# A hybrid attention layer on one core: PSUM banks of the level products given back 1.2 planned microseconds later, and the order of small products that follows

## The chip, the cores and the metric

The kernel runs on one core of one Trainium2 chip. The time is device microseconds for one execution. Three runs of the kernel before gave 207.26, 206.81 and 206.92 us, median 206.92. One more execution was profiled: it took 207.39 us, and its span (first to last instruction of the trace) is 205.6 us, so 1.8 us lie around the span.

## The reference

One decoder layer on 256 tokens of width 1024. The input is normalised (RMS) and multiplied by a wide matrix `w_in` whose columns are split into parts; two branches follow and are merged by gates:

```
h = rms_norm(x, norm_in_g[layer])
proj = jnp.einsum('bsd,de->bse', h, w_in[layer])
(mq, mk, mv, mgate, gq, gk, gv, ggate, gfg, ga, gb) = jnp.split(proj, split_pts, axis=-1)
...
oa = moba_attention(qa, ka, va)          # 8 heads of 64, causal softmax over 256 keys
oa = oa * silu(mgate);  ya = oa @ w_proj_a
...
ob = gla_chunked(qb, kb, vb, gdec)       # 4 heads, decay per channel, chunks of 64
ob = rms_norm(ob) * silu(ggate);  yb = ob @ w_proj_b
merged = sigmoid(ga + b0) * ya + sigmoid(gb + b1) * yb
out = rms_norm(x + merged @ w_out)
```

With 256 tokens there is one block of keys, so the first branch is plain causal attention. In the second branch the weight between two positions of a chunk is a sum over channels of q, k and a decay, which the kernel builds from six levels of block products (block sizes 32 down to 1) and the diagonal.

## The kernel before, in words

Large products. All weights come as 512 KB chunks. `load_to` (L170) issues a chunk's DMA into one of 5 raw buffers, `split_to` (L183) splits it on ScalarE into a high part (`hi`, L193) and on VectorE into the rest (`lo`, L194), each in one of 5 buffers, and `three` (L724) multiplies high by high, high by low and low by high. Splits run 4 chunks ahead of TensorE, loads up to 8. The groups are computed in a fixed order: mg, gg, gqk, mq, mk, mv, gv, ga, gb, then pa and pb (the two projections), then po (the output). Products of gv are 512 columns wide, those of ga and gb 256.

Small products. Two Python generators run beside the large groups. `gla()` (L368) makes the second branch: the level products `a` (L459, in two passes over the levels, the loop of L439), then `b` (L477), `c` (L492), `o` (L506) and the transposes `tr` (L528). `scores()` (L539) is started four times, once for each pair of heads: products `sc` (L548), mask and maximum on VectorE (L556), exponentials on ScalarE (L563), division on VectorE (L569), transposes `pt` (L577), a copy back on ScalarE (L581), and the products `pv` (L594).

The order. The program that is built is one fixed list of instructions for each engine; no scheduler changes it. A planned clock (L139) is advanced by each large product, and a generator that yields a number is resumed when that many planned microseconds, times 0.9, have passed. Two rules decide when a small product may be written into the list. First, `together()` (L331) holds small products back until several ask or one has waited long enough (L662), so that they stand in blocks between large products. Second, the small products share four PSUM banks, counted in `room` (L318): `take("small", 2)` (L320) holds a generator until two are free, `give` (L325) frees them. This count exists at planning time alone. On the chip a bank is handed on by semaphores: the first product in a bank waits until the engine that read its last contents is done.

What reads a bank: `a` is copied out on VectorE by predicated copies (L468), `sc` by VectorE (L556), `b` by ScalarE (L482), `c` by ScalarE (L495), `pt` by ScalarE (L581), `o` by ScalarE and VectorE (L512, L520).

Of the kernel before, what the change touches and what calls it, by code (L numbers as in the profile page):

```python
# [130 lines left out]
def layer(ctx, tc, x, xT, columns, weights, w_fg2, b_fg, gla_g, norm_f_g, rope, causal, sums, masks, out):  # L131
# [9 lines left out]
    def mm(out, lhsT, rhs, start, stop):  # L141
        nc.tensor.matmul(out, lhsT, rhs, start=start, stop=stop)  # L142
        n = out.free_size() / 2400
        clock[0] += n if rhs.dtype == F32R else 4 * n
# [14 lines left out]
    def small(name):  # L159
        return bank(name, "small", 4)  # L160
# [159 lines left out]
    def take(tag, n=1):  # L320
        while room[tag] < n:
            yield 0.3
        room[tag] -= n

    def give(tag, n=1):  # L325
        room[tag] += n
# [4 lines left out]
    def together(weight=1):  # L331
        me = [weight, clock[0]]
        company["ask"].append(me)
        while not company["open"]:
            yield 0
        company["ask"].remove(me)
# [31 lines left out]
    def gla():  # L368
# [44 lines left out]
        def halves(ap, n, which):  # L413
            return ap.rearrange("p g (b h j) -> p g b h j", h=2, j=n)[:, :, :, which, :]

        def upper(ap, l):
            return ap.rearrange("p (b h j) -> p b h j", h=2, j=LEVELS[l])[:, :, 1, :]
# [21 lines left out]
        for levels in ((0, 1, 2, 3), (4, 5, NL)):  # L439
            yield from take("small", 2)  # L440
            yield from together(2)
            banks = [small(f"a{r}") for r in range(2)]
            at, cuts = 0, []
            for l in levels:
                width = CH // 2 if l < NL else CH
                cuts.append([bk[:, at:at + 4 * width].rearrange("p (g t) -> p g t", t=width) for bk in banks])
                at += 4 * width
            for l, a in zip(levels, cuts):
                for g, (t, ct) in enumerate(order):
                    for par in range(2):  # L450
                        c = 2 * t + par
                        for r in range(2):
                            rows = halves64[r]
                            if l < NL:
                                lhs = EX[rows, ct, l, c * CH:(c + 1) * CH]
                                rhs = upper(lhs, l)
                            else:
                                lhs, rhs = gkT[rows, ct, c * CH:(c + 1) * CH], gqT[rows, ct, c * CH:(c + 1) * CH]
                            mm(a[r][halves64[par], g, :], lhs, rhs, start=True, stop=True)  # L459
            yield 0.6  # L460
            for l, a in zip(levels, cuts):
                for r in range(2):
                    to, mask, new = ATr[:, r], masksb[:, l:l + 1, :].to_broadcast([P, 4, CH]), a[r]
                    if l < NL:
                        j = LEVELS[l]
                        to, mask = halves(to, j, 1), halves(mask, j, 1)
                        new = new.rearrange("p g (b j) -> p g b j", j=j)
                    nc.vector.copy_predicated(to, mask, new)  # L468
            give("small", 2)
            yield 1  # L470
        ready.add("levels")
        yield from take("small", 2)
        yield from together()
# [197 lines left out]
    def wait_for(*names):  # L671
        while not all(n in ready for n in names):
            wait(0.3)

    start_side(gla())
    start_side(attention())

# [225 lines left out]
```

## Time and profile before

| | |
|---|---|
| median of three runs | 206.92 us (206.81 to 207.26) |
| profiled execution | 207.39 us, span 205.6 us |
| TensorE (PE) busy | 195.0 us, 95% of the span |
| VectorE (DVE) busy | 141.2 us, 69% |
| ScalarE (ACT) busy | 123.4 us, 60% |
| GpSimd (POOL) busy | 38.1 us, 19% |
| mean DMA rate | 177 GB/s |
| chain that ended last: PE | 58% of the span |

A matmul row lasts from its start to the modelled end of a pipelined operation, so rows of PE overlap, and a busy share of 95% doesn't say how fast one follows the other. The distance from one start to the next does. A wait is shown in brackets behind a row, with the engine and line that ended it. A matmul of plain fp32 shows as two rows, so four products `sc` are eight rows.

### The profile page before, as it was taken

What the parts mean: (1) busy time and instruction counts of PE and PEld (TensorE: products, weight loads), DVE (VectorE), ACT (ScalarE), POOL (GpSimd) and SP (SyncE); (2) the same over time, 40 slices, a digit from 0 to 9 for tenths busy, and PEclk for the clock granted to TensorE, in tenths of its full rate; (3) what the DMA queues carried; (4) which work ended last, traced back from release to release, by engine and by line L of the source; (5) the groups of instructions that cost most, each with busy time, mean ns of one, the idle gap of its engine ahead of it and who ended that gap; (6) DMA issues with size and microseconds to landing.
All of it is one profiled execution on the core that took longest, in us unless ns stands there. A gap on an engine that the chain in (4) does not pass through costs nothing.

```text
span 205.6 us, 4197 instructions
## 1 busy us (share of the span) xinstructions
PE 195.0 (95%) x1666; PEld 179.0 (87%) x1666; DVE 141.2 (69%) x259; ACT 123.4 (60%) x205; POOL 38.1 (19%) x31
## 2 busy tenths in 40 slices
PE   7999978999999999989999999999999999999970
PEld 3899968899999887867789999999999999989870
DVE  3776278969655999989567448945284959755471
ACT  6685657865999956058774729756436553552251
POOL 2000034800412579002000001100010060420011
PEclk9999999999999999999999999999999999999997
DMA  6999986484546446542333372756363683500022
GB/s 175 332 407 398 346 319 205 141 296 148 168 138 205 125 183 204 175 139 100 108 102 100 119 256 69 287 198 207 102 202 108 207 298 110 204 0 5 0 102 102
DMA packets 12245, 36.44 MB, mean 177 GB/s; under 512 B 1457, under 2 KB 2882, under 8 KB 12226
## 3 DMA queue, kind: packets, MB, share of 16 engines
q1 hardware_dynamic: 11794, 35.64, 51.2%
q10 hardware_dynamic: 432, 0.54, 0.7%
q8 instruction: 13, 0.21, 0.4%
q14 instruction: 6, 0.05, 0.1%
HBM read 35.12 MB, written 1.05 MB: 176 GB/s over the span
## 4 chain that ended last, share of the span: by engine, by line
PE 58%; DVE 12%; ACT 11%; DMA 8%; issue 6%; SPq 2%; POOL 1%; POOLq 0%; DVEq 0%; ACTq 0%
PE ga L142 11%; PE gb L142 11%; PE po L142 8%; PE gqk L142 6%; PE pa L142 5%; PE pb L142 5%; DVE lo L194 5%; DMA xt<-in_x_dram 5%; ACT hi L193 4%; ACT z L705 3%; DMA first<-in_weights_dram 3%; PE mq L142 3%; PE gv L142 2%; DVE EX L422 2%; ACT EX L405 2%
## 5 line engine op out<-in xcount | busy, mean ns | idle before, releaser
L194 DVE TENSOR_TENSOR lo<-raw,hi 128x1024 fp32r<-128x1024 f32 (+1 forms) x56 | 70.7, 1270 | 30.2 <-ACT hi L193 30.1
L193 ACT CAST hi<-raw 128x1024 fp32r<-128x1024 f32 (+1 forms) x56 | 57.9, 1048 | 21.6 <-PE po L142 6.0
L142 PE MATMUL ga<-xh,hi 128*128 128x256 f32 x64 | 18.1, 283 | 0.0
L142 PE MATMUL gb<-xh,hi 128*128 128x256 f32 x64 | 18.1, 282 | 0.0
L142 PE MATMUL gb<-xl,hi 128*128 128x256 f32 x64 | 17.9, 279 | 0.0
L142 PE MATMUL gb<-xh,lo 128*128 128x256 f32 x64 | 17.9, 279 | 0.0
L142 PE MATMUL ga<-xh,lo 128*128 128x256 f32 x64 | 17.8, 278 | 0.0
L142 PE MATMUL ga<-xl,hi 128*128 128x256 f32 x64 | 17.8, 278 | 0.0
L142 PE MATMUL po<-hi,ml 128*128 128x512 f32 (+1 forms) x40 | 13.9, 347 | 0.0
L142 PE MATMUL po<-lo,mh 128*128 128x512 f32 (+1 forms) x40 | 13.8, 346 | 0.0
L142 PE MATMUL po<-hi,mh 128*128 128x512 f32 (+1 forms) x40 | 13.7, 343 | 0.0
L142 PEld LDWEIGHTS ga<-xh,hi 128*128 128x128 f32 x64 | 12.1, 189 | 0.5 <-issue 0.5
L516 POOL TENSOR_TENSOR s<-s,mhalf 128x4 f32<-128x4 f32 x2 | 2.3, 1170 | 54.6 <-DVE s L515 54.6
L563 ACT ACTIVATE sm<-sm,mx 128x128 f32<-128x128 f32 (+1 forms) x16 | 7.1, 443 | 8.7 <-DVE mx L558 8.6
L142 PEld LDWEIGHTS gb<-xh,lo 128*128 128x128 f32 x64 | 12.1, 189 | 0.0
L142 PEld LDWEIGHTS gb<-xh,hi 128*128 128x128 f32 x64 | 12.1, 189 | 0.0
L142 PEld LDWEIGHTS ga<-xl,hi 128*128 128x128 f32 x64 | 12.0, 188 | 0.0
L142 PEld LDWEIGHTS gb<-xl,hi 128*128 128x128 f32 x64 | 12.0, 188 | 0.0
L142 PEld LDWEIGHTS ga<-xh,lo 128*128 128x128 f32 x64 | 12.0, 188 | 0.0
L709 POOL TENSOR_TENSOR kT<-kT,z 128x512 f32<-128x512 f32 x2 | 10.5, 5234 | 7.2 <-DVE z L708 7.2
L629 POOL TENSOR_TENSOR m<-m,sa 128x512 f32<-128x512 f32 x4 | 7.0, 1744 | 23.9 <-DVE m L627 22.0
L142 PE MATMUL gqk<-xh,hi 128*128 128x256 f32 x32 | 9.2, 286 | 1.0 <-DVE mgz L359 1.0
(189 smaller groups left out, 599.5 us busy)
## 6 DMA issues: line engine op xcount, KB each, us to landing
raw<-in_weights_dram SPq DMA_DIRECT2D x52, 512.0 KB, 3.4
raw<-in_weights_dram SPq DMA_DIRECT2D x4, 528.0 KB, 7.4
first<-in_weights_dram SPq DMA_DIRECT2D x8, 256.0 KB, 5.4
xt<-in_x_dram SPq DMA_DIRECT2D x2, 512.0 KB, 9.9
xs<-in_xT_dram SPq DMA_DIRECT2D x3, 256.0 KB, 5.2
late<-in_norm_f_g_dram SPq DMA_DIRECT2D x1, 512.0 KB, 4.1
out_dram<-late SPq DMA_DIRECT2D x2, 256.0 KB, 2.0
out_dram<-late ACTq DMA_DIRECT2D x2, 256.0 KB, 2.5
```

The costliest lines, as they stand in the source:

```text
L142: nc.tensor.matmul(out, lhsT, rhs, start=start, stop=stop)
L193: nc.scalar.copy(c["hi"], raw)
L194: nc.vector.tensor_sub(c["lo"], raw, f32(c["hi"]))
L405: nc.scalar.activation(EX[:, ct, :, c * CH:(c + 1) * CH], e.rearrange("p (l t) -> p l t", t=CH), AF.Exp, scale=1.0 / 16)
L422: nc.vector.tensor_mul(e, e, halves(src, LEVELS[l], which))
L516: nc.gpsimd.tensor_tensor(s4, s4, mhalf, op=OP.pow)
L563: nc.scalar.activation(sm[i][:, cs], sm[i][:, cs], AF.Exp, bias=mx[:, i, t:t + 1], scale=0.125, accum_out=den[:, i, t:t + 1])
L629: nc.gpsimd.tensor_add(m, m, cut(sg["ga"]))
L705: nc.scalar.copy(z[i:i + 32], p2[i ^ 32:(i ^ 32) + 32])
L709: nc.gpsimd.tensor_add(dst, dst, z)
```

## The change

In the loop over the two passes of level products, the two banks were given back as soon as their copies were issued, and the generator then yielded 1 planned microsecond. Now it yields 1.2 first and gives the banks back afterwards.

```
                     nc.vector.copy_predicated(to, mask, new)
+            yield 1.2
             give("small", 2)
-            yield 1
         ready.add("levels")
```

No instruction is added, removed or altered in shape; the number of TensorE rows is the same. What differs is where small products stand among the large ones, from the second pass of the levels on.

TensorE, behind the second pass: the third block of small products. `pt` are the transposes of one pair of heads, `sc` the scores of a later pair, `gv_1036` and `gv_1037` the two banks of the group gv. Before:

```order
L142 MATMUL gv_1036<-hi,xl 128x512
L147 MATMUL pt<-ident,sm 128x128 x6
L142 MATMUL sc_1267<-kT,qT 128x128
L142 MATMUL sc_1268<-kT,qT 128x128
L142 MATMUL sc_1267<-kT,qT 128x256
L142 MATMUL sc_1268<-kT,qT 128x256
L142 MATMUL gv_1037<-hi,xh 128x512
```

That block stood behind 6 products of gv. It is gone from there; all 27 remaining products of gv now follow one another, then 6 of ga, and only then comes a block, with `b` ahead of `pt`. The place now (between the rows of `b` and of ga shown there are more of the same):

```order
L142 MATMUL gv_1037<-hi,xl 128x512
L142 MATMUL ga_1296<-xh,hi 128x256
...
L142 MATMUL b_1309<-QP,KS 64x64
L142 MATMUL b_1310<-QP,KS 64x64
...
L147 MATMUL pt<-ident,sm 128x128 x6
L142 MATMUL ga_1296<-xh,hi 128x256
```

From there on the blocks are composed anew. Before: [pt sc] [b pv pt] [pv pt sc] [c pv pt] [o pv] [tr] [o] [tr]. Now: [b pt] [pt sc] [c pv pv sc] [o pt] [pv pt] [tr pv] [o] [tr]. There are eight in both, and pa, pb and po are as they were.

ScalarE, at the same place: `gv` are the copies of the group gv (L695), `hi` the casts of weight chunks, `ATf<-b` the copies that empty the banks of `b`, `sm<-pt` those that empty the banks of `pt`.

```order
 L563 ACTIVATE sm,den<-sm,mx 128x128
 L563 ACTIVATE sm,den<-sm,mx 128x256
-L581 COPY sm<-pt 128x384 x2
+L193 CAST hi<-raw 128x1024
+L695 ACTIVATE gv<-gv_1036,rs 128x512
+L695 ACTIVATE gv<-gv_1037,rs 128x512
+L193 CAST hi<-raw 128x1024
+L482 COPY ATf<-b_1309 64x4x64
+L482 COPY ATf<-b_1310 64x4x64
+L581 COPY sm<-pt 128x384 x4
+L193 CAST hi<-raw 128x1024
```

The copies of `b` and of `pt` now stand behind two casts and the two copies of gv, and before the exponentials of the third pair of heads.

VectorE, at the same place: `lo` are the second halves of the splits, the reciprocals and the two lines of L569 behind each finish the softmax that the `pt` of the second pair needs.

```order
 L558 TENSOR_SCALAR mx<-mx 128x2
-L194 TENSOR_TENSOR lo<-raw,hi 128x1024
-L556 ISA sm,mx<-sc_1267,causalt 128x128
...
+L194 TENSOR_TENSOR lo<-raw,hi 128x1024 x2
+L567 RECIPROCAL den<-den 128x2
+L569 TENSOR_SCALAR sm<-sm,den 128x128
+L569 TENSOR_SCALAR sm<-sm,den 128x256
```

A second `lo` stands ahead of that softmax now, where one `lo` and the masks of the third pair stood.

## Rows read from the trace of the kernel before

**Rows 1.** Chain that ended last, from 93 us on: start, length (us), what

```profile
93.62 0.92 PE sc L142 x4
...
104.94 7.02 PE ga L142 x60
...
123.40 7.26 PE ga L142 x60
130.66 5.66 PE gb L142 x48
...
161.13 5.44 PE pb L142 x48
...
177.45 16.47 PE po L142 x84
```

**Rows 2.** Timeline of TensorE, 89 to 105 us: start, length (us), operation, [idle before]

```profile
89.59 0.50 PE L142 MATMUL gv<-hi,xh 128*128 128x512 f32 x1
...
90.86 0.40 PE L142 MATMUL gv<-hi,xl 128*128 128x512 f32 x1
92.11 0.85 PE L147 MATMUL pt<-ident,sm 128*128 128x128 f32 x6 [0.85 <-DVE AT L468]
92.96 0.46 PE L142 MATMUL sc<-kT,qT 64*128 64x128 f32 x2
93.62 0.92 PE L142 MATMUL sc<-kT,qT 64*128 64x128 f32 x6 [0.20 <-DVE mx L556]
94.47 0.50 PE L142 MATMUL gv<-hi,xh 128*128 128x512 f32 x1
...
97.78 0.40 PE L142 MATMUL gv<-hi,xl 128*128 128x512 f32 x1
98.11 0.68 PE L142 MATMUL b<-QP,KS 64*64 64x64 f32 x16
98.72 0.87 PE L142 MATMUL pv<-sm,mv 128*64 128x256 f32 x8
99.52 0.88 PE L147 MATMUL pt<-ident,sm 128*128 128x128 f32 x6
100.15 0.47 PE L142 MATMUL gv<-hi,xh 128*128 128x512 f32 x1
...
101.61 0.28 PE L142 MATMUL ga<-xh,hi 128*128 128x256 f32 x1
...
102.41 0.87 PE L142 MATMUL pv<-sm,mv 128*64 128x256 f32 x8
...
104.02 0.93 PE L142 MATMUL sc<-kT,qT 64*128 64x128 f32 x8
104.87 0.38 PE L142 MATMUL ga<-xh,hi 128*128 128x256 f32 x1
```

**Rows 3.** Timeline of ScalarE, 94 to 104 us

```profile
94.82 0.83 ACT L581 COPY sm<-pt 128x384 f32<-128x384 f32 x2
...
97.55 1.03 ACT L193 CAST hi<-raw 128x1024 fp32r<-128x1024 f32 x1
98.87 0.63 ACT L482 COPY ATf<-b 64x256 f32<-64x256 f32 x2 [0.29 <-PE b L142]
...
101.13 1.37 ACT L695 ACTIVATE gv<-gv,rs 128x512 f32<-128x512 f32 x2 [0.16 <-PE gv L142]
102.40 1.04 ACT L193 CAST hi<-raw 128x1024 fp32r<-128x1024 f32 x1
```

**Rows 4.** Timeline of VectorE, 93 to 98 us

```profile
93.77 1.21 DVE L194 TENSOR_TENSOR lo<-raw,hi 128x1024 fp32r<-128x1024 f32 x1
...
96.40 0.16 DVE L567 RECIPROCAL den<-den 128x2 f32<-128x2 f32 x1
...
97.25 0.55 DVE L569 TENSOR_SCALAR sm<-sm,den 128x128 f32<-128x128 f32 x2
```

**Rows 5.** One stretch: length, busy PE, PEld, DVE, ACT, POOL, PEclk, DMA, GB/s

```profile
92.00:94.60 2.60, 2.28 (x15) 1.57 (x16) 2.53 (x12) 1.55 (x7) 1.59 (x4) 1.00 0.00 0
```

More of the change, by code (lines that the diff above doesn't have):

```diff
@@ L468, in gla @@
                     nc.vector.copy_predicated(to, mask, new)
+            yield 1.2
             give("small", 2)
-            yield 1
         ready.add("levels")
```

## The prediction

> **What bounds the kernel now.** I read the chain of waits first. From 93.62 us on it runs on TensorE alone, through the rest of gv, ga, gb, pa, pb and into po at 177.45 us [rows 1]; no later row of TensorE's timeline up to the end of pa and pb carries a wait. So every microsecond that TensorE loses before or in that stretch moves the end by as much, and what the other engines do counts only where TensorE waits for it. Then the timeline of TensorE around 90 us, where the change begins to move rows. There two waits stand next to each other: 0.85 us ahead of `pt`, ended by the predicated copies of the levels (L468), and 0.20 us in the middle of `sc`, ended by VectorE's maximum (L556) [rows 2]. Both are waits for a bank. `pt` was written into the list six large products behind the second pass of `a`, because the planner had given the banks of `a` back on issuing their copies, while on the chip those copies were still running; `sc` then wants the banks of the pair before it.
>
> **What the two waits cost.** The brackets add up to 1.05 us, but they count from modelled ends. I go by starts, each against the same step elsewhere in rows 2.
> - Last gv to `pt`: 90.86 to 92.11 is 1.25 us. Last gv to `b`, with nothing awaited: 97.78 to 98.11, 0.33. Lost: 0.92.
> - `pt` to `sc`: 92.11 to 92.96 is 0.85. Undisturbed, `pv` and `pt` take 1.61 together (102.41 to 104.02), of which `pv` is 0.80 (98.72 to 99.52), so `pt` is 0.81. Lost: 0.04.
> - `sc` to the next large product: 92.96 to 94.47 is 1.51, against 0.85 (104.02 to 104.87). Lost: 0.66, three times the bracket. The reason lies in the row counts: two rows had started alone at 92.96, and the other six, from 93.62 on, take the whole 0.85 again.
>
> The sum is 1.62 us. [...]
>
> **What the change takes away.** The block [pt sc] no longer stands there. TensorE has 27 products of gv and 6 of ga to do while VectorE finishes the copies, so I count the whole 1.62 as removed, if nothing else is late. That has to be followed through the next blocks, with lengths from rows 2.
> - Products of gv: 14 distances from 94.47 to 97.78 make 3.31, 13 more at 0.23 make 3.0, so ga begins at 89.59 + 6.3 = 95.9. Six of ga with the step into a block take 0.80 (101.61 to 102.41): `b` at 96.7. Its banks are those of `a`, whose copies were done when the bracket ended, at 92.11 [rows 2]: no wait.
> - `b` is 0.61 (98.11 to 98.72), so `pt` of the first pair stands at 97.3; its banks were read by the maximum that ended the wait at 93.62: no wait. `pt` before a large product is 0.63 (99.52 to 100.15), six of ga with both steps 0.9: second `pt` at 98.8, its second bank 0.4 later at 99.2, `sc` at 99.6.
>
> **What is late next.** ScalarE is now the giver of banks: second `pt` takes the banks of `b`, `sc` those of the first `pt`. On ScalarE the queue ahead is longer than it was. It is free at 94.82, when before it took up `pt` [rows 3]. Now come a cast, about 1.0 (to 95.8), the two copies of gv, 1.27 (101.13 to 102.40; gv is done at 96.0, in time for the second), to 97.1, another cast to 98.1, the two copies of `b`, 0.63 in all, to 98.4 and 98.75, and the two of `pt`, 0.83, to 99.2 and 99.6 [rows 3]. Against 98.8 and 99.2 for the second `pt` the spare time is 0.4 and 0.45; against 99.6 and 99.7 for the two halves of `sc` it is 0.4 and 0.1. The casts' chunks lie in their buffers: from 92.0 to 94.6 no DMA moves anything [rows 5], and loads run ahead of splits.
>
> VectorE has a second `lo` ahead of the softmax of the second pair. The first `lo` is 1.21 from 93.77, the second can start with the end of the cast, 95.85, and ends at 97.05; reciprocals and divisions of both heads took 1.40 (96.40 to 97.80) [rows 4], so they end at 98.45, and the first head's at 97.75. Needed: 99.2 and 98.8. Spare: 0.75 and more. So I expect no wait, at the most a few tenths at `sc`.
>
> Further on every reader has more time: `c` stands 18 products of ga behind `sc` and needs only the copies of the second `pt`; `o` stands behind 54 products of ga, some 6 us after `c`; `tr` 66 products behind. Of the loads, the order on SyncE's queue is unchanged, and the splits that free their buffers come earlier or at the same point of the large products as before.
>
> **Terms that the trace shows only in part.** The blocks are eight as before and hold the same products, so stepping in and out costs the same. `pt` costs 0.81 ahead of `sc` and 0.63 ahead of a large product; before, two of four stood ahead of `sc`, now one: -0.18. Three new neighbours (`b` to `pt`, `o` to `pt`, `tr` to `pv`) have no row; from the 0.10 that a step from gv into a block costs over the ordinary 0.23, they cost at most 0.1 each. Between -0.2 and +0.1, taken as 0.
>
> The pace of the large products isn't uniform. 60 of ga take 7.02 us behind a block that ends in `sc`, 7.26 behind one that ends in `pv`; 48 of gb take 5.66 where 48 of pb take 5.44 [rows 1]. That is 4 to 4.6 ns a product. Before, the slow stretches are 108 products behind [o pv] and 78 behind [o]; behind `sc`, `pt` and `tr` it is fast. If the last kind of small product sets it, 66 behind [tr pv] and 108 behind [o] are slow now: 174 in place of 186, -0.05 us. I don't know the cause, so the bounds are all 384 products of ga and gb at one pace or the other: 198 more slow ones, +0.85, or 186 fewer, -0.8. I take -0.05, the value by kind, since every stretch of the trace fits it.
>
> [...]
>
> **Sum.** -1.62 - 0.05 = -1.67 us. The profiled execution took 207.39 (span 205.6 and 1.8 around it), which makes 205.7; it stood 0.47 above the median of the runs. From the median of 206.92 it is 205.3 us.
>
> **Rivals.**
> - *A part comes back at the next bank.* If each of the five steps on ScalarE takes 0.15 to 0.2 longer than I put it, the copies of `pt` end 0.75 to 1.0 later, and `sc` waits 0.6 or more of it. Time 205.9. For: the spare of 0.1 at the second half of `sc`. Against: each length is a row's.
> - *The gap was no loss to the end.* TensorE would reach a later point 1.67 us sooner and wait there, for weights or for the gates: 206.9. For: the weights of gb, pa, pb and po are all still to be loaded. Against: their loads wait for buffers that TensorE's progress frees, and nothing on the way has a bracket now.
> - *Slower: the bank behind ScalarE's queue.* The cast ahead of the copies of `b` ran only at 102.40 before [rows 3]. Were it held until then by its data, it would end at 103.45, the copies of `b` at 104.1, and the second bank of `pt`, wanted at 99.2, would wait 4.9 us: 205.3 + 4.9 = 210.2. The change becomes a loss from the point where those copies end 1.67 us after 99.2, at 100.9, which is 2.1 us later than in my sum. [...] Against the rival: no transfer was under way at 94.6, and the row at 102.40 follows directly on the copies of gv that stood ahead of it.
> - *The change doesn't do what it says* (TensorE waits for the banks of `a` all the same) is excluded: `b` takes them at 96.7, over 4 us after the last copy.
>
> **How the numbers follow.** The forecast as it stands 0.70, a part back 0.16, no change 0.08, slower 0.06. Pace and neighbours move the first case between 204.5 and 206.2 at the extremes. I set the range from 204.7 to 206.4, which holds the first two cases but for their outer ends. About 0.2% (0.4 us) is what a measurement of this kernel can tell from no change. Faster than that: 0.70 + 0.15 = 0.85. Within it 0.08 and the last hundredth of the second case: 0.09. Slower 0.06.
>
> **What the new profile would show.** Right: 27 products of gv without a bracket from 89.6 to 95.9; `b` at 96.7, `sc` at 99.6 without a bracket; pa beginning near 153.7 instead of 155.4. Part back: a bracket of some tenths at the second `pt` or at `sc`, ended by ScalarE L482 or L581. Wrong on pace: ga or gb at the slow pace behind `pt`, `tr` or `sc`, or at the fast one behind `pv` or `o`. No change: a bracket of over a microsecond in gb, pa, pb or po that isn't there now. The whole argument would be wrong if the start of pa moved by 1.6 us and the time did not.

## The result and the profile after

The median of 20 runs is 204.87 us (204.31 to 207.16). The twenty runs of the kernel before that stand beside them have the median 207.16 us. The ratio is 0.9896 (95% interval 0.9881 to 0.991): the change is worth 2.29 us between the medians. The forecast was 205.3 us, from a gain of 1.67 us. The time lies in the forecast's range, near its lower end. The profiled execution of the changed kernel took 204.66 us, with a span of 202.9 us.

From the page of the changed kernel: the busy time and share of each engine, then the share of the chain that ended last.

```profile
PE 194.2 (96%) x1666; PEld 179.4 (88%) x1666; DVE 141.6 (70%) x259; ACT 122.6 (60%) x205; POOL 38.9 (19%) x31
...
PE 79%; DMA 10%; issue 3%; DVE 2%; SPq 2%; POOL 1%; ACT 1%; POOLq 0%; ACTq 0%
```

TensorE's share of the chain rose from 58% to 79%, while its busy time fell by 0.8 us only. A busy share of 95 or 96% said nothing of what was to be had. These are all the waits of TensorE that the changed kernel's trace shows (engine, tile and line, what was waited for: us in total, times, longest):

```profile
PE idle L253 <- DVE zero L239: 1.2, 1, 1.2
PE gqk L142 <- DVE mgz L359: 0.9, 1, 0.9
PE mg L142 <- DVE lo L194: 0.2, 1, 0.2
```

They all belong to the start. The waits at `pt` and `sc` [rows 2] are gone, and none took their place. TensorE's timeline at the place of the change:

```profile
95.29 0.40 PE L142 MATMUL gv<-hi,xl 128*128 128x512 f32 x1
95.53 0.28 PE L142 MATMUL ga<-xh,hi 128*128 128x256 f32 x1
...
96.31 0.68 PE L142 MATMUL b<-QP,KS 64*64 64x64 f32 x16
96.93 0.87 PE L147 MATMUL pt<-ident,sm 128*128 128x128 f32 x6
97.56 0.37 PE L142 MATMUL ga<-xh,hi 128*128 128x256 f32 x1
...
98.34 0.82 PE L147 MATMUL pt<-ident,sm 128*128 128x128 f32 x6
99.08 0.93 PE L142 MATMUL sc<-kT,qT 64*128 64x128 f32 x8
99.94 0.39 PE L142 MATMUL ga<-xh,hi 128*128 128x256 f32 x1
```

ScalarE, which had to empty the banks of `b` and of the first `pt` in time, in the changed kernel:

```profile
94.44 1.03 ACT L193 CAST hi<-raw 128x1024 fp32r<-128x1024 f32 x1
95.38 1.25 ACT L695 ACTIVATE gv<-gv,rs 128x512 f32<-128x512 f32 x2
96.53 1.04 ACT L193 CAST hi<-raw 128x1024 fp32r<-128x1024 f32 x1
97.46 0.63 ACT L482 COPY ATf<-b 64x256 f32<-64x256 f32 x2
97.99 1.73 ACT L581 COPY sm<-pt 128x384 f32<-128x384 f32 x4
```

The start-up differs from one profiled execution to the next: the first `a` starts between 81.12 us (no_copies_after) and 83.03 (yield_0p6) in kernels whose lists are the same up to there. So the stretch that the change touches is compared from the first start of the first pass of `a` to the first start of `pa`. Before it takes 73.51 us (81.91 to 155.42), after 71.28 (81.48 to 152.76): 2.23 less, nearly all of the 2.29. The chain that ended last, of the changed kernel (start, length, what; its starts are some 0.1 to 0.2 later than the timeline's; compare [rows 1]):

```profile
89.29 6.39 PE gv L142 x27
...
102.91 1.45 PE pv L142 x16
...
111.55 0.89 PE o L142 x8
112.44 0.66 PE pt L147 x6
...
116.76 7.50 PE ga L142 x66
124.26 0.44 PE tr L147 x4
124.70 0.80 PE pv L142 x8
125.50 2.94 PE ga L142 x24
128.43 4.76 PE gb L142 x42
133.19 1.78 PE o L142 x16
134.98 12.72 PE gb L142 x108
...
148.14 4.78 PE gb L142 x42
152.92 5.44 PE pa L142 x48
```

The pace can be read from these rows. 108 products of gb in 12.72 us are 117.8 ns each. 66 of ga in 7.50 (behind [pv pt]) are 113.6, 42 of gb in 4.76 are 113.3. These 42, with the 24 of ga ahead of them, are the 66 products behind [tr pv]; they run at the fast pace, and the prediction had put them down as slow.

### The profile page after: what moved, and what is told of

Read it like the earlier page. It is cut to its first block, busy times and chain, and to the rows that moved or that the text cites. A ratio compares the mean times of both kernels' runs of the same rounds, so it can differ in the third digit from the quotient of the medians.

```text
span 202.9 us, 4197 instructions
## 1 busy us (share of the span) xinstructions
PE 194.2 (96%) x1666; PEld 179.4 (88%) x1666; DVE 141.6 (70%) x259; ACT 122.6 (60%) x205; POOL 38.9 (19%) x31
## 3 DMA queue, kind: packets, MB, share of 16 engines
HBM read 35.12 MB, written 1.05 MB: 178 GB/s over the span
## 4 chain that ended last, share of the span: by engine, by line
PE 79%; DMA 10%; issue 3%; DVE 2%; SPq 2%; POOL 1%; ACT 1%; POOLq 0%; ACTq 0%
PE ga L142 11%; PE gb L142 11%; PE po L142 8%; PE gv L142 6%; PE gqk L142 6%; PE mk L142 6%; PE mq L142 5%; PE mv L142 5%; PE pb L142 5%; PE pa L142 5%; DMA xt<-in_x_dram 4%; DMA raw<-in_weights_dram 3%; DMA first<-in_weights_dram 3%; PE a L142 2%; PE sc L142 2%
## 5 line engine op out<-in xcount | busy, mean ns | idle before, releaser
L516 POOL TENSOR_TENSOR s<-s,mhalf 128x4 f32<-128x4 f32 x2 | 2.9, 1474 | 44.3 <-DVE s L515 44.3
```

Of the source, the lines that this page charges most:

```text
L516: nc.gpsimd.tensor_tensor(s4, s4, mhalf, op=OP.pow)
```

## The experiments

Each kernel's time stands beside runs of the kernel before on its own chip. The ratio is that of the runs on record with its interval; it isn't the quotient of the two medians beside it. The last column is the first `a` to the first `pa` in the profiled execution, of which there is one for each kernel.

| kernel | median us (runs) | before there | ratio (95%) | `a` to `pa` |
|---|---|---|---|---|
| before | | | | 73.51 |
| after | 204.87 (20) | 207.16 | 0.9896 (0.9881 to 0.991) | 71.28 |
| no_copies_before | 205.56 (10) | 207.31 | 0.993 (0.9903 to 0.9958) | 71.82 |
| no_copies_after | 204.55 (4) | 207.31 | 0.9878 (0.9854 to 0.9902) | 71.24 |
| transpose_after_o | 204.70 (4) | 207.31 | 0.9887 (0.987 to 0.9904) | 71.38 |
| fp32_after_o | 204.78 (6) | 207.14 | 0.9882 (0.9846 to 0.9917) | 70.97 |
| bf16_after_o | 205.01 (6) | 207.14 | 0.9899 (0.9857 to 0.994) | 71.44 |
| yield_0p6 | 205.53 (7) | 207.14 | 0.9918 (0.9886 to 0.995) | 72.21 |
| yield_1p6 | 205.39 (4) | 206.98 | 0.9889 (0.9824 to 0.9954) | 71.80 |
| yield_2p5 | 207.86 (10) | 207.14 | 1.0039 (1.0014 to 1.0063) | 74.02 |

### The wait alone: the second pass's copies left out

In no_copies_before and no_copies_after the six predicated copies of the second pass are left out, so the weights of the last levels are missing from the output. The lists of all other instructions stay as they are. Lines behind L468 count one more.

```
-                    nc.vector.copy_predicated(to, mask, new)
+                    if levels[0] == 0:
+                        nc.vector.copy_predicated(to, mask, new)
```

no_copies_before, as expected ahead of it:

> The kernel before, in its own order of instructions, without the six predicated copies (L468) of the second pass of the levels; that part of the result is left out. It takes away what `pt` and `sc` wait for at 92 and 93.6 us and moves nothing else on TensorE. Theory: the two waits cost 1.62 us by starts, so last gv to `pt` falls from 1.25 to 0.33 us, `sc` to the next large product from 1.51 to 0.85, pa starts 1.6 us nearer to the block's first gv (64.2 us after it instead of 65.8), and the time falls by 1.6 us, ratio 0.992. Rival 1: only the brackets, 1.05 us, ratio 0.995. Rival 2: the whole gain of the change is the wait, 2.2 us, ratio 0.9895.

Measured: 205.56 us. TensorE's timeline of no_copies_before, where [rows 2] has the two waits:

```profile
90.67 0.39 PE L142 MATMUL gv<-hi,xl 128*128 128x512 f32 x1
90.90 0.81 PE L147 MATMUL pt<-ident,sm 128*128 128x128 f32 x6
91.65 0.95 PE L142 MATMUL sc<-kT,qT 64*128 64x128 f32 x8
92.53 0.50 PE L142 MATMUL gv<-hi,xh 128*128 128x512 f32 x1
```

Last gv to `pt` is 0.23 where it was 1.25, `pt` to `sc` 0.75 where it was 0.85, `sc` to gv 0.88 where it was 1.51: 1.02 + 0.10 + 0.63 = 1.75 us. From the first gv of this stretch to `pa` the kernel is 1.75 shorter than before (64.08 against 65.83). So the whole loss of the two waits reaches the end, and none of it comes back. The brackets, 1.05 us, would have given 60% of it. The changed kernel is 0.54 us quicker still in this stretch; that part isn't the wait.

no_copies_after:

> The changed kernel without the same six copies. Theory: they are off TensorE's path now, since `b` takes their banks 4 us after the last one, so nothing but VectorE's own rows move: ratio to the kernel before 0.9895, the same as the changed kernel, within 0.1%. Rival: the copies still delay something by up to their 1.9 us of VectorE (the softmax of the second pair, or a split); then it is up to 0.9% faster than the changed kernel.

Measured: 204.55 us, `a` to `pa` 71.24 against 71.28; the intervals of the two ratios overlap. In the changed order the copies can go or stay: TensorE doesn't meet them any more.

### How far the give is moved: 0.6, 1.6 and 2.5 planned microseconds

Of the edit, the place of the give alone sets the order: written as give and then `yield 1.2`, the list of TensorE is the one of before; written as `yield 1` and then give, it is the changed one, row for row. Between 0.8 and 1.4 ahead of the give the list stays the same. Three values outside were run.

```
-            yield 1.2
+            yield 0.6        (yield_0p6; 1.6 and 2.5 in yield_1p6 and yield_2p5)
             give("small", 2)
```

yield_0p6:

> The changed kernel with 0.6 instead of 1.2 planned microseconds ahead of the give. The second pass of `a` then stands 6 instead of 9 products of gv behind the first `sc`, and `b` and the third `sc` form one block 30 products of gv later. By the theory that only banks handed on late cost TensorE time: the second pass of `a` would start at 85.93 instead of 86.62, but its banks are free only when the first pass's copies end, 86.5 to 86.6 in the changed kernel's trace; so a bracket of 0.3 to 0.6 at `a`, ended by VectorE at L468, and all behind it 0.6 to 0.7 later: 205.4 to 205.6. Rival (it is the give behind the yield that counts, not the place it leads to): 204.9, the time of the changed kernel, and no bracket at `a`.

Measured: 205.53 us. TensorE, at the second pass of `a`:

```profile
87.14 0.40 PE L142 MATMUL gv<-hi,xl 128*128 128x512 f32 x1
88.09 1.28 PE L142 MATMUL a<-EX 64*64 64x32 f32 x62 [0.56 <-DVE AT L468]
```

The wait for the copies came back one pass earlier, as worked out: 0.95 us from gv to `a` instead of 0.33. That is 0.62 of the 0.93 us that `a` to `pa` is longer than in the changed kernel. A second bracket of 0.20 us, which wasn't expected, stands at `pt`. The rival fell: here too the give stands behind the yield, and a wait is there all the same. What counts is where the products then stand. Most of the gain is kept (205.53 against 207.14 before).

yield_2p5:

> The changed kernel with 2.5 instead of 1.2 planned microseconds ahead of the give. The second pass of `a` stands 15 products of gv behind the first `sc`; behind it come 21 of gv, 12 of ga, [b sc], 12 of ga, and both `pt` in one block. By the theory of banks: `a` at 88.0, its banks long free; `b` at 96.9, banks of `a` copied out by 93.3; third `sc` 97.5; `pt` 99.8, its third bank wanted at 100.6 and read out by the masks 1.6 us behind the start of that `sc`, 99.1. No bracket anywhere, so the time of the changed kernel, 204.9, within 0.3 for the pace and the make-up of blocks. Rival (1.2 is needed for itself, other values bring other waits): a bracket of over 0.3 at `pt` or `sc`, 205.3 or more.

Measured: 207.86 us, slower than before. Here my expectation failed. TensorE's rows with a wait, in yield_2p5:

```profile
100.88 0.88 PE L147 MATMUL pt<-ident,sm 128*128 128x128 f32 x6 [0.66 <-ACT ATf L482]
102.79 0.55 PE L147 MATMUL pt<-ident,sm 128*128 128x128 f32 x3 [1.03 <-DVE mx L556]
103.53 0.55 PE L147 MATMUL pt<-ident,sm 128*128 128x128 f32 x3 [0.20 <-DVE mx L556]
```

I had followed TensorE's products and taken VectorE's order for unchanged. It isn't. VectorE in yield_2p5 (the rows that matter):

```profile
90.50 1.23 DVE L194 TENSOR_TENSOR lo<-raw,hi 128x1024 fp32r<-128x1024 f32 x1 [2.12 <-ACT hi L193]
...
92.97 1.93 DVE L468 COPY_PREDICATED AT<-masksb,a 128x128 f32<-128x128 int32 x6
...
98.50 1.23 DVE L194 TENSOR_TENSOR lo<-raw,hi 128x1024 fp32r<-128x1024 f32 x1 [2.02 <-ACT hi L193]
```

and in the changed kernel:

```profile
89.97 1.93 DVE L468 COPY_PREDICATED AT<-masksb,a 128x128 f32<-128x128 int32 x6
```

Since the second pass is written into the list six products later, a `lo` stands ahead of its copies. That `lo` waits for its cast on ScalarE, which stands behind the exponentials of the first pair. Counted from the first `a` (81.75 in yield_2p5, 81.48 in the changed kernel), the copies start at 11.22 instead of 8.49, which is 2.73 us later, and with them all that follows in the two queues is late. ScalarE in yield_2p5:

```profile
95.66 0.40 ACT L563 ACTIVATE sm<-sm,mx 128x128 f32<-128x128 f32 x1 [5.19 <-DVE mx L558]
...
100.47 0.63 ACT L482 COPY ATf<-b 64x256 f32<-64x256 f32 x2
```

Counted in the same way, the copies of `b` are 2.74 us later than in the changed kernel (100.47 and 97.46). Two casts and the copies of gv, which need nothing of the softmax, stood behind the exponentials, which waited 5.19 us. (The copies of gv lost little of that: gv itself is done at about 95.6.) In this trace ScalarE starts them in the order of its list: the exponentials from 95.66 on, a cast at 97.44, the copies of gv at 98.37, a cast at 99.53, the copies of `b` at 100.47. The masks of the third pair, which empty the banks that the second half of `pt` wants, stand on VectorE behind the next `lo`, and that one waits for its cast on ScalarE in turn (the row at 98.50).

From `a` to `pa` the loss against the changed kernel is 2.74 us as well, but TensorE pays it at more than one place. yield_0p6 has the same blocks [b sc] and [pt pt] with 12 products of ga between them, so the starts can be set side by side. From those 12 products to `pt` it is 2.30 us against 1.49: 0.81 lost, at the wait that ScalarE ended. The block of two `pt` is 2.96 against 1.70: 1.26 lost, at the waits that VectorE's masks ended. From there to the end of `c` it is 3.37 against 2.88: 0.49. So the prediction's slower rival, the bank behind ScalarE's queue, is at work here in another order, but directly it is the smaller part; the larger one is a bank behind VectorE's queue, which ScalarE holds up.

yield_1p6 was chosen to tell apart whether it is that `lo` or the block of two `pt` close behind [b sc]:

> The changed kernel with 1.6 instead of 1.2 planned microseconds ahead of the give. TensorE's blocks are those of the changed kernel up to six products of ga ([b pt], six of ga, [pt sc]); but on VectorE the copies of the second pass now stand behind one `lo`, as with 2.5. Theory (with 2.5 the loss came from that `lo`: the masks of the second pair, the exponentials behind them and everything queued on ScalarE slipped by its length and its wait for the cast): copies from about 91.5 instead of 89.97, exponentials from 94.2 instead of 92.67, the copies of `b` about 1.5 later than in the changed kernel, 99.0 instead of 97.46; the second `pt`, wanted at 98.4, waits 0.6 to 1.2 for them or for its division, and `sc` 0 to 0.3 more: 205.6 to 206.4. Rival (with 2.5 the loss came from the block of two `pt` 12 products of ga behind [b sc], which isn't here): no bracket over 0.2, 204.9.

Measured: 205.39 us, between the rival's 204.9 and the theory's 205.6 to 206.4. Rows of TensorE, ScalarE and VectorE of yield_1p6, in this order:

```profile
100.13 0.87 PE L147 MATMUL pt<-ident,sm 128*128 128x128 f32 x6 [0.23 <-ACT ATf L482]
```

```profile
99.71 0.64 ACT L482 COPY ATf<-b 64x256 f32<-64x256 f32 x2
```

```profile
91.07 1.23 DVE L194 TENSOR_TENSOR lo<-raw,hi 128x1024 fp32r<-128x1024 f32 x1 [0.19 <-ACT hi L193]
```

The `lo` alone, with the blocks of the changed kernel, makes the copies of `b` 1.40 us later, counted from the first `a` (82.33 here): 17.38 against 15.98. That is close to the 1.5 expected, and the wait at `pt` came with it, though with a bracket of 0.23 us and not 0.6 to 1.2, barely above the 0.2 of the rival. The loss from `a` to `pa` is 0.52 us, less than the 0.7 to 1.5 I had worked out, because `b` itself stands 0.54 later on TensorE: six more products of ga are done ahead of it, and that time isn't lost. By starts, the steps from ga to `pt` and from `sc` to ga take 0.51 and 1.06 where the changed kernel has 0.12 and 0.86, 0.59 in all. So the rows show the `lo` ahead of the copies as a cause of a wait; they are those of one profile, and the times alone can't tell this kernel from the changed one (0.9889, interval 0.9824 to 0.9954, beside 0.9896). In yield_2p5 the `lo` stands ahead of the divisions too and waits 2.12 us, and there the block of two `pt` wants four banks at once, the last two of which wait for masks that are late for the same reason. yield_0p6 takes the two apart: it has that block too, but no `lo` between the masks of the first pair and the copies of the second pass, and its only bracket in the block is the 0.20 us. So the block alone costs little; what yield_2p5 loses beyond that comes with the late copies.

### The pace of the large products

Theory K, for kind, is the prediction's: the kind of the last small product sets the pace of the large products behind it. Rival P, for place: some stretches of the program are slow whatever stands ahead. In pace_after_e six of the eight products `e`, which stand in the groups mq and mk, get one more product behind them, each of another form; its result is read by nobody. In transpose_after_o a transpose is put behind the second `o`.

```
                 mm(e, gs[:, c % 2, c // 2, ct * P:(ct + 1) * P], sumsr, start=True, stop=True)
+                n = ct * NC + c
+                if n == 0:
+                    extra = bank("extra", "side", 1)
+                if n == 1:
+                    nc.tensor.transpose(extra[:, :P], ident, ident)
...
+                if n == 6:
+                    nc.tensor.matmul(extra[:, :S], xh[:, 0, :P], xh[:, 1, :], start=True, stop=True)
```

> The changed kernel with one extra small product (its output unused) behind the single product `e` in six of its eight places: none, transpose 128x128, fp32 128x128, fp32 with 64 rows of weights, fp32 with 64 columns of weights, bf16 128x512, split product 128x256, none. In the kernel before the 256-column products behind every `e` follow at 117.7 ns. Theory K (the kind of the last small product but `pv` sets the pace of the stretch): 113.3 ns behind the transpose, and behind the one with 64 rows, as behind `pt`, `tr` and `sc`; 117.7 behind the fp32 128x128 (as behind `o`), the 64 columns (as `pv` behind `o`), the split product and none. Rival P (the pace is fixed by the place in the program or by what other engines do there): 117.7 in all eight. Rival A (any extra product shifts it by chance): a mix without relation to the kind.

Measured (one run, 206.8 us; the pace is read from its trace). Distances in ns between the last starts of the large products behind `e` and the product named:

```
changed kernel, behind each e  119 117 118 118 118 117   slow
transpose, 128x128             113 113 114 113 113 114   fast
fp32, 128x128                  114 113 113 114 113 113   fast
fp32, 64 rows of weights       118 118 117 118 118 117   slow
fp32, 64 columns of weights    114 113 113 114 113 113   fast
bf16, 512 columns              113 114 113 113 114 113   fast
split, 256 columns             113 114 113 113 114 113   fast
nothing (the last e)           118 117 118 118 118 117   slow
```

Both K and P fell. Weights of 64 rows, the form of `sc`, gave the slow pace here, where `sc` in the program is followed by the fast one; weights of 64 columns, the form of `pv`, gave the fast one, where the stretch behind [o pv] was slow. And the same places were slow without the extra product and fast with it: all eight places behind `e` are slow in the profiles of the kernel before and of the changed kernel (a mean of 117 to 118 ns from the fourth start on), five of the six with an extra product are fast here (113 to 114). What is left is a mix without relation to the kind, the outcome that rival A named; that it comes about by chance is another matter, taken up below.

> The changed kernel with one extra transpose 128x128 (output unused) behind the second block of `o`, ahead of 108 products of gb that follow at 117.7 ns. Theory K: they follow at 113.3 ns, -0.47 us, less 0.1 to 0.2 for the transpose: pa starts 0.3 us earlier than in the changed kernel; time ratio to before 0.988. Rival P: pace unchanged, 0.1 to 0.2 us slower than the changed kernel, ratio 0.990.

Measured: 204.70 us, the same as the changed kernel within the intervals. The transpose made nothing fast, so K falls here again. Two more products at this place followed, with the same edit and another line in it (the one of fp32_after_o is shown; bf16_after_o has `pvs[1], zero[:, :P], zero` in it):

```
                 mm(oo, ATf[:, h % 2, t * 2 + h // 2, :], vals["GV"][:, t, h * P:(h + 1) * P], start=(t == 0), stop=True)
+            if t:
+                nc.tensor.matmul(pvs[1][:, :P], ident, ident, start=True, stop=True)
```

> The changed kernel with one more product, plain fp32 128x128, behind the second `o` (its result goes into a bank and is read by nobody). In the changed kernel the 108 products of gb behind [o16] step at 117.7 ns; one more transpose there left them at 117.7. Theory (the exact sequence of the step into the stretch picks one of two paces, 113.3 or 117.7 ns, and a fp32 product behind `e` was followed by the fast one): 113.3 here as well, 108 x 4.4 ns = -0.48, the product itself +0.1 to +0.25, pa at 152.4 to 152.55 by the scale on which the changed kernel has 152.76, time 204.5 to 204.65. Rival (this stretch is slow whatever stands ahead of it): 117.7 ns, pa 0.1 to 0.25 later, time 205.0 to 205.1.

> The same with a product of 512 columns in bf16 in place of the fp32 one, of which the next product behind `e` was also followed by the fast pace. Theory: 113.3 ns, -0.48 + 0.2 to 0.3, time 204.6 to 204.7. Rival (slow whatever stands ahead): 117.7 ns, time 205.05 to 205.2. If one of the two extra products gives the fast pace and the other doesn't, neither kind nor place sets it and only the rows say which it will be.

The chain of transpose_after_o:

```profile
134.94 0.11 PE pv L509
135.05 12.72 PE gb L142 x108
```

of fp32_after_o:

```profile
135.84 0.22 PE pv L509 x2
136.06 12.26 PE gb L142 x108
```

and of bf16_after_o:

```profile
135.32 0.22 PE pv L509
135.54 12.72 PE gb L142 x108
```

Behind the fp32 product alone the pace is fast, 12.26 us for the 108 products of gb. The product costs 0.22 and the pace gives 0.46 back, and the stretch from `a` to `pa` is the shortest of all, 70.97 us. The median, 204.78, can't be told from the changed kernel's 204.87, so this isn't shown to be a better version. The 512 columns in bf16, fast behind `e`, leave the pace slow behind `o`. What in the sequence decides stays open, and so does whether the sequence alone does. From the change on, the stretches of 18 products or more were alike in every profile of one order: the 108 products behind the second `o` are slow (117.8 ns) in all six profiles that have that order without an extra product, those behind `sc` and `tr` are fast (113.1 to 113.8). But the first 24 products of gqk, which stand ahead of everything that any of these edits moves, took 3.00 us in the changed kernel, as in the kernel before, both at a granted clock of 1.00, and 3.09 in no_copies_before, whose mean clock over the span is 0.991. The changed kernel, then no_copies_before:

```profile
30.98 3.00 PE gqk L142 x24
```

```profile
31.10 3.09 PE gqk L142 x24
```

The 0.09 us are 3.8 ns for each of the 24, near the 4.4 between the two paces; but the mean doesn't tell the clock of that stretch, and a lower one there would lengthen it too. The six products of ga behind [b pt], in the changed order, take 0.46 us from the second start to the last in three profiles (the changed kernel, no_copies_after, bf16_after_o) and 0.47 in three (transpose_after_o, fp32_after_o, pace_after_e), which differ by no more than the last digit of the rows. So that the same list can give either pace is likely and not shown. With one profile for each extra product, that an extra product can change the pace is well supported behind `e`; that the fp32 product, and not chance, did it behind `o` isn't shown.

## Why the prediction was right, and where it was short

- *The two waits.* Right in place, cause and size. Worked out as 1.62 us by starts, measured as 1.75 by taking the copies away. The 0.13 is in the comparison used: last gv to `b` is 0.33, and I took this for the step to `pt` as well, which is 0.23 when nothing is awaited; the undisturbed `pt` ahead of `sc` is 0.75 and not 0.81.
- *No new wait.* Right. `b` at 96.31 was forecast for 96.7 and `sc` at 99.08 for 99.6; the first gv came 0.37 earlier in this execution, which is most of that. ScalarE's copies of `b` began at 97.46, where the forecast had 98.1. The rival of the slower bank had its 6% for a mechanism that exists: with a later give (yield_2p5) TensorE does wait for a bank behind ScalarE's queue (a bracket of 0.66 us at `pt`), though it lost more at banks behind VectorE's masks, which that rival doesn't name. At 1.2 neither comes about.
- *The pace.* This term failed in its rule, and the bounds held it. The 66 products behind [tr pv] were put down as slow "by kind" and are fast. So 108 products are slow and not 174. Against 186 before that is 78 x 4.4 ns = -0.34 us, where -0.05 was taken. That it fell on the good side is luck: the bounds reached from -0.8 to +0.85, and no rule is known that would have told which.
- *The make-up of the blocks.* Taken as 0 between -0.2 and +0.1, and it came out at that lower bound. What is left of the difference to no_copies_before is 0.54 - 0.34 = 0.20 us. The rows agree roughly: the two `pv` that now stand together take 1.45 where two apart take 1.61; four `pt` take 2.58 us in all where no_copies_before has 2.82; `o` is 0.89 ahead of `pt` and 0.98 ahead of `pv`; the `tr` ahead of `pv` is 0.18 dearer than the one ahead of a large product. That makes -0.16 - 0.24 - 0.09 + 0.18 = -0.31, with 0.1 of it given back in the steps around the blocks.
- *The start of pa* came at 152.76, where 153.7 was forecast: 0.43 of that is an earlier start of the whole stretch in this execution, which has nothing to do with the change, and the rest is what the waits, the pace and the make-up gave beyond the forecast.

The sum by the profiles is -1.75 - 0.34 - 0.20 = -2.29 from the first gv on; the last term is what was left over, so it adds up by itself. That the medians differ by 2.29 too is the check from outside. So three quarters of the gain are the mechanism that was forecast, and the rest are two terms that the prediction could only bound.

## What to carry to other kernels

Size a wait by the distance of starts against the same step elsewhere, not by its bracket: here 1.75 us stood behind 1.05 us of brackets. In `sc`, the six rows behind the stall took the 0.85 us that all eight take undisturbed. When a planning constant is moved, follow every engine's list around it and not that of the bound engine alone: one `lo` ahead of six copies cost 0.5 us in yield_1p6, and, further ahead of them and with a block that wants four banks soon after, the whole gain in yield_2p5. And such a constant has a window: here the list is the same from 0.8 to 1.4, while the values below and above that were run brought other waits.

## What the runs showed of the hardware

The split products of 256 columns ran at one of two paces, 113.3 or 117.7 ns from start to start, in one execution, both at a granted clock of 1.00 (the changed kernel, 101 to 112 us and 135 to 147 us). From the fifth product behind a block to the next block the pace holds: of the 108 slow products in one stretch (12.72 us) the first half steps at 117.6 ns on the mean and the second at 117.9, of the 66 behind [pv pt] at 113.3 and 113.2 (the changed kernel). From the change on, the stretches of 18 products or more had the same pace in every profile of the same order. Whether the list alone fixes it isn't shown: the first 24 products of gqk took 3.00 us in the changed kernel, at a clock of 1.00, and 3.09 in no_copies_before, with 0.991 over its span. Behind `e`, five of six extra products were followed by the fast pace (113 to 114 ns), at places that are slow (117 to 118) in the kernel before and in the changed one; behind the second `o`, one of three was (12.26 us for 108 products, against 12.72).

The wait inside the group of plain fp32 products `sc` cost more than its bracket: 0.20 us of bracket were 0.63 us by starts, measured by taking the wait away (no_copies_before).
